# Key and value projections of a fused decoder layer in pairs of seven block products instead of eight, both values ahead of the second HGRN2 head

## The chip, the cores and the metric

One core of a Trainium2 chip runs the whole program in one launch. The metric is the time of that launch in microseconds (us). Times are medians of runs; a profiled execution is one run with the hardware profiler, and its trace gives start and length of every instruction. The engines are TensorE (PE, matrix products; PEld are its weight loads), VectorE (DVE), ScalarE (ACT), GpSimd (POOL) and SyncE (SP, which here issues nearly all transfers).

## The reference, cut to what matters

One layer of a hybrid decoder for 512 prompt tokens and 8 x 4 sample tokens (the sample tokens with caches of 2048 positions). All 544 tokens share the weights:

```
h = rmsnorm(x, norm_mix)
z = h @ w_in                                   # 1024 -> 3 * 512 + 4 * 512
aq, ak, av, hq, hf, hi, hg = split(z)
att = head_rmsnorm(dilated_attention(aq, ak, av))     # 8 heads of 64
o   = hgrn2_recurrence(silu(hq), 1 - f, hi, log f)    # 4 heads of 128
x = x + concat([att, head_rmsnorm(o) * silu(hg)]) @ w_out
x = x + cross_attention(rmsnorm(x), memory)
x = x + (silu(causal_conv3(u @ w_gate)) * (u @ w_up)) @ w_down    # u = rmsnorm(x), 2816 wide
return rmsnorm(x), new keys, new values, states
```

All is in float32. The change is in the products that make `ak` and `av`, two of the seven parts of `z`.

## The kernel before

Activations lie with features on the partitions and the 544 tokens along a row. A float32 product is made of three passes in a faster 32-bit format (`float32r`): every operand is split into a high part (ACT casts it) and a low part (DVE subtracts the high part from the original), and `passes` issues high x high, high x low and low x high, dropping low x low. For the norm's input these are `xs` (`xm0h`, `xm0l` to `xm7h`, `xm7l`, 128 features each, already times the gain `norm_mix`); the division by the norm's root, `r_mix`, is done when a result is evacuated, so projections can start before the norm is known.

A projection makes one tile of 128 output columns (two attention heads or one HGRN2 head): `proj_in` calls `dense`, which takes the next weight tile (`wr` raw, `wh` high, `wl` low, 1024 x 128 numbers as 8 blocks), and does the tokens in two halves, `CUTS`: 256 and 288 columns. Each half has a PSUM bank from `PD` (two banks), 8 x 3 matmuls and an evacuation on DVE by `proj_evac`. Behind each half `sides.pump()` lets one step of the side work be issued: the sample tokens' attention over the caches (`decode_attention`, whose tiles `st` come from memory through five buffers, with products `psd` for scores and `psdo` for values) and later the memory's input. Other small PSUM tiles come from `PX` (five banks). The softmax and value products of the prompt's attention (`prompt_attention`, tiles `psS`, `P`, `PT`, `psT`, `psO`) follow a value tile; `hgrn` follows the four projections of a head, with many small steps over levels of 1 to 64 tokens (`kq`, `hf`, `hG`, `psA`, `psB`, `psL`).

The order of the mixer is a tuple:

```
MIX_ORDER = (("h", 0), ("q", 0), ("q", 1), ("q", 2), ("q", 3), ("k", 0), ("k", 1), ("k", 2), ("k", 3), ("v", 0),
             ("h", 1), ("v", 1), ("h", 2), ("v", 2), ("h", 3), ("v", 3))
```

It is the order of writing alone. `tile_decoder_step` does not issue instructions: a recording layer, `Tape`, takes every instruction with an estimated length, groups them into steps, and `Tape.order` lays the steps out for each engine by a simulation with due times. The projections are the main line, in the order written (`tape.main()`); all else is put between them as it becomes ready and due, at most so far ahead as a gate on the main line allows. `tape.early(lead)` gives the steps within it an earlier due time. Because every instruction passes through one helper, nearly all rows of the profile have the line L723, and transfers L695; pieces of work are known by the names of their tiles. In the profile a tile's number is left out (`wl`, not `wl7`).

The feed-forward part, later, already does pairs of weight tiles with seven block products instead of eight (class `Pair`, banks `ps_a`, `ps_c`, `ps_d`, copies `kept`, sums `S1` to `S4` of weight blocks and `X`, `T`, `U`, `V` of token blocks). The mixer does not.

## Time and profile before

| | us |
|---|---|
| median of 3 runs | 821.66 (821.13 to 822.02) |
| the profiled execution | 821.08 |
| its span in the trace | 819.3 |
| PE busy | 808.6 |
| DVE busy | 594.8 |
| ACT busy | 421.3 |
| POOL busy | 152.9 |

The granted PE clock was 0.997 over the span. The span runs from the first to the last instruction; the execution's time is 1.8 us longer. Busy time counts overlapping instructions of one engine once. In the trace's rows the first number is the start in us from the span's beginning, the second the length; "[0.47 <-ACT keptu L723]" means that the engine was idle for 0.47 us ahead and that ACT's work on `keptu` ended this. The mixer's projections and side work fill the time from about 24 to 280 us, the feed-forward part that from about 442 us on.

### The profile page before, as it was taken

How to read it: one execution, taken by the hardware profiler on the slowest of the kernel's cores; microseconds unless marked ns; L12 is line 12 of the kernel's file. 1: busy time of each engine (PE TensorE's matmuls, PEld its weight loads, DVE VectorE, ACT ScalarE, POOL GpSimd, SP SyncE). 2: the span in 40 equal slices, each digit the busy share in tenths (PEclk: the TensorE clock that was granted, in tenths of full speed). 3: DMA queues.
4: the chain of work that ended last, by engine and by line, in shares of the span. 5: the costliest groups of instructions: out<-in, count | busy, mean ns of one | idle time of the engine just before them, and what ended most of it. 6: DMA issues, size and time to landing. Idle time of an engine off the chain costs nothing.

```text
span 819.3 us, 18836 instructions
## 1 busy us (share of the span) xinstructions
PE 808.6 (99%) x7545; PEld 761.3 (93%) x7545; DVE 594.8 (73%) x1252; ACT 421.3 (51%) x838; POOL 152.9 (19%) x246
## 2 busy tenths in 40 slices
PE   9999999999999999999999999999999999999996
PEld 9998988987998789999889999999999999999995
DVE  6785534965787996573589999876677767879983
ACT  7413533634636646353555565554455544666553
POOL 1130000110120310231133331121020212221023
PEclk9999999999999999999999999999999999999998
DMA  8657779696942544252733374556455645776603
GB/s 311 214 143 219 261 233 312 210 320 210 304 131 91 188 134 153 78 173 73 222 126 112 66 190 129 136 139 176 122 141 149 165 126 130 180 193 169 147 4 110
DMA packets 93639, 137.04 MB, mean 167 GB/s; under 512 B 6512, under 2 KB 60656, under 8 KB 93552
## 3 DMA queue, kind: packets, MB, share of 16 engines
q1 hardware_dynamic: 86496, 123.77, 47.5%
q0 software_dynamic: 6336, 11.54, 8.9%
q8 instruction: 59, 0.97, 0.5%
q10 hardware_dynamic: 720, 0.53, 0.2%
q14 instruction: 28, 0.23, 0.1%
HBM read 127.75 MB, written 8.07 MB: 166 GB/s over the span
## 4 chain that ended last, share of the span: by engine, by line
PE 95%; ACT 1%; DVE 1%; DMA 1%; SPq 0%; issue 0%; DVEq 0%
PE ps_d L723 9%; PE ps_au L723 7%; PE ps_ag L723 7%; PE ps_wo L723 6%; PE ps_cu L723 4%; PE ps_cg L723 3%; PE ps_k L723 3%; PE ps_q L723 3%; PE ps_hv L723 3%; PE ps_g L723 3%; PE ps_cq L723 3%; PE ps_v L723 3%; PE ps_dz L723 3%; PE ps_co L723 3%; PE ps_az L723 2%; PE ps_hq L723 2%
## 5 line engine op out<-in xcount | busy, mean ns | idle before, releaser
L723 ACT CAST wh<-wr 128x1024 fp32r<-128x1024 f32 (+1 forms) x68 | 59.4, 883 | 100.9 <-PE ps_q L723 15.4
L723 DVE TENSOR_TENSOR wl<-wr,wh 128x1024 fp32r<-128x1024 f32 (+1 forms) x68 | 71.6, 1062 | 8.3 <-ACT wh L723 7.7
L723 POOL TENSOR_TENSOR hG<-hG,hf 128x256 f32<-128x256 f32 (+1 forms) x28 | 24.4, 870 | 185.6 <-DVE hf L723 86.5
L723 POOL COPY last<-ug 128x2 f32<-128x2 f32 (+1 forms) x44 | 21.0, 500 | 128.0 <-DVE ug L723 107.3
L723 DVE TENSOR_TENSOR xr<-xr,ps_d 128x256 f32<-128x256 f32 (+1 forms) x48 | 20.9, 436 | 29.9 <-PE ps_d L723 29.8
L723 DVE SCALAR_TENSOR_TENSOR cv<-ug,vec,cv 128x560 f32<-128x560 f32 x44 | 35.1, 798 | 3.7 <-ACT cv L723 3.1
L723 ACT ACTIVATE cv<-cv 128x560 f32<-128x560 f32 x22 | 14.8, 673 | 17.8 <-DVE cv L723 17.7
L723 POOL TENSOR_TENSOR acc_cx<-acc_cx,sq_cx 128x256 f32<-128x256 f32 (+1 forms) x14 | 11.7, 837 | 58.5 <-ACT sq_cx L723 58.4
L723 ACT ACTIVATE P<-P,mx 128x128 f32<-128x128 f32 (+3 forms) x32 | 17.6, 553 | 9.1 <-DVE mx L723 8.9
L723 ACT ACTIVATE cv<-ug,vec 128x560 f32<-128x560 f32 x22 | 18.8, 857 | 4.2 <-DVE ug L723 3.2
L723 POOL COPY ug<-conv_state 128x16 f32<-128x16 f32 x22 | 17.3, 787 | 15.4 <-PE ps_au L723 9.1
L723 PE MATMUL ps_co<-coh,wh 128*128 128x256 f32 (+1 forms) x64 | 19.2, 300 | 0.1
L723 DVE TENSOR_TENSOR xr<-xr,ps_wo 128x256 f32<-128x256 f32 (+1 forms) x16 | 6.8, 436 | 16.3 <-PE ps_wo L723 16.3
L723 PE MATMUL ps_co<-col,wh 128*128 128x256 f32 (+1 forms) x64 | 18.4, 288 | 0.0
L695 POOL DMA_DIRECT2D S1u<-in_w_up x10 | 8.8, 877 | 51.7 <-DVE cv L723 26.2
L723 PE MATMUL ps_co<-coh,wl 128*128 128x256 f32 (+1 forms) x64 | 18.4, 288 | 0.0
L723 DVE TENSOR_TENSOR up<-ps_cu,keptu 128x272 f32<-128x272 f32 x20 | 8.7, 437 | 11.5 <-PE ps_cu L723 11.2
L723 PE MATMUL psd<-st,qbd_win 128*32 128x224 f32 x256 | 15.5, 358 | 0.0
L723 DVE CUSTOM_DVE_ANT_0 P<-psS,bias 128x128 f32<-128x128 f32 (+3 forms) x32 | 14.3, 485 | 1.2 <-PE psS L723 1.2
L723 POOL TENSOR_TENSOR acc_ux<-acc_ux,sq_ux 128x256 f32<-128x256 f32 (+1 forms) x13 | 11.3, 871 | 20.3 <-ACT sq_ux L723 20.1
L723 PE MATMUL psdo<-st,dpt 128*32 128x256 f32 x224 | 14.8, 385 | 0.0
L723 ACT ACT_TABLE_LOAD x11 | 14.1, 1283 | 1.4 <-PEq L2531 1.2
(2610 smaller groups left out, 3596.8 us busy)
## 6 DMA issues: line engine op xcount, KB each, us to landing
st<-in_kwT SPq DMA_DIRECT2D x32, 448.0 KB, 5.6
st<-in_vw SPq DMA_DIRECT2D x28, 512.0 KB, 6.5
wr<-in_w_in SPq DMA_DIRECT2D x25, 512.0 KB, 5.2
wd<-in_w_down SPq DMA_DIRECT2D x24, 256.0 KB, 3.2
wru<-in_w_up SPq DMA_DIRECT2D x10, 512.0 KB, 5.1
wrg<-in_w_gate SPq DMA_DIRECT2D x9, 512.0 KB, 4.9
st<-in_mkT SPq DMA_DIRECT2D x8, 512.0 KB, 5.2
wr<-in_w_out SPq DMA_DIRECT2D x8, 512.0 KB, 3.8
```

The costliest lines, as they stand in the source:

```text
L695: return tape.put(engine, lambda: call(*args, **kw), outs, ins, 0.1, 0.3, size)
L723: return tape.put(engine, lambda: call(*args, **kw), outs, ins, length, lag, size, port, codes, work, mode)
```

## The change

Two things. First, the mixer's order: keys 2 and 3 become one entry, values 0 and 1 become one, and both values stand ahead of the second HGRN2 head; value 1 stood behind that head.

Second, an entry with two tiles goes through `proj_pair`. With the two weight tiles as rows (A11 and A12: the two halves of the inner dimension of the first tile, A21 and A22: of the second) and the normed input as blocks (B11, B12: the first 512 features for tokens 0 to 271 and 272 to 543; B21, B22: the other 512 features), the 2 x 2 block product is made from seven products of 128 x 512 by 512 x 272, each 4 x 3 matmuls of 272 columns, in place of eight. The other operands are sums: S3 = A11 + A21, S1 = A21 + A22, S2 = S1 + A11 and S4 = S2 + A12 of weights, and X = B12 - B22, T = B11 - B12, U = X - B11 and V = B21 + U of tokens. Banks: a and c are the two `PD` banks, d comes from `PX`, and gets one marking matmul that opens its accumulation. ACT copies three partial results out of bank a while they are still to be added to (to d, to `z`, to `r`). `make_blocks` makes the token sums once, written after the first query tile with a lead of 30 us: ACT scales the eight input tiles by `norm_mix`, DVE makes 16 differences of 272 columns, ACT and DVE split them. `take_pair` makes the weight sums: four DVE adds of 512 columns, and five splits of 512, beside the first tile's split of 1024, as before.

The diff, cut to its core:

```diff
-MIX_ORDER = (("h", 0), ("q", 0), ("q", 1), ("q", 2), ("q", 3), ("k", 0), ("k", 1), ("k", 2), ("k", 3), ("v", 0),
-             ("h", 1), ("v", 1), ("h", 2), ("v", 2), ("h", 3), ("v", 3))
+MIX = (('h', 0), ('q', 0), ('q', 1), ('q', 2), ('q', 3), ('k', 0), ('k', 1), ('k', 2, 3), ('v', 0, 1), ('h', 1), ('h', 2), ('v', 2), ('h', 3), ('v', 3))
+PREPARE, LEAD_X = 2, 30.0
...
+        def take_pair(self, name):
+            top = self.take()
+            raw = self.raw[self.i - 1][0]
+            a11, a12 = raw[:, 0:4, :], raw[:, 4:8, :]
+            t = {n: A(f"{n}_{name}", [128, 4, 128]) for n in ("S3", "S1", "S2", "S4")}
+            self.load(self.i)
+            low = self.raw[self.i][0]
+            self.i += 1
+            a21, a22 = low[:, 0:4, :], low[:, 4:8, :]
+            sums = (("S3", a11, a21), ("S1", a21, a22), ("S2", t["S1"], a11), ("S4", t["S2"], a12))
+            found = {"A11": top[0:4], "A12": top[4:8]}
+            for n, a, b in sums:
+                nc.vector.tensor_tensor(t[n], a, b, op=ALU.add)
+            for n, src in (("S3", t["S3"]), ("S2", t["S2"]), ("S1", t["S1"]), ("S4", t["S4"]), ("A22", a22)):
+                hi, lo = (A(f"{n}{p}_{name}", [128, 4, 128], F32R) for p in "hl")
+                nc.scalar.copy(hi, src)
+                nc.vector.tensor_tensor(lo, src, hi.bitcast(F32), op=ALU.subtract)
+                found[n] = [(hi[:, k, :], lo[:, k, :]) for k in range(4)]
+            return found
...
+    mix_blocks = {}
+    def make_blocks():
+        for j, name in enumerate(("B11", "B21", "B12", "B22")):
+            c0 = HT * (j // 2)
+            mix_blocks[name] = [tuple(t[:, c0:c0 + HT] for t in xs[4 * (j % 2) + k]) for k in range(4)]
+        for k in range(KT):
+            nc.scalar.activation(xin[k][:, :N], xin[k][:, :N], AF.Copy, scale=V("norm_mix", k))
+        for kp in range(2):
+            made = {n: A(f"x{n}{kp}", [128, 2, HT]) for n in "XTUV"}
+            for i in range(2):
+                top, low = xin[2 * kp + i], xin[4 + 2 * kp + i]
+                b11, b12, b21, b22 = top[:, :HT], top[:, HT:N], low[:, :HT], low[:, HT:N]
+                x_, t_, u_, v_ = (made[n][:, i, :] for n in "XTUV")
+                for out, a, b, op in ((x_, b12, b22, ALU.subtract), (t_, b11, b12, ALU.subtract),
+                                      (u_, x_, b11, ALU.subtract), (v_, b21, u_, ALU.add)):
+                    nc.vector.tensor_tensor(out, a, b, op=op)
+            for n in "XUTV":
+                hi, lo = (A(f"x{n}{p}{kp}", [128, 2, HT], F32R) for p in "hl")
+                nc.scalar.copy(hi, made[n])
+                nc.vector.tensor_tensor(lo, made[n], hi.bitcast(F32), op=ALU.subtract)
+                mix_blocks.setdefault(n, []).extend((hi[:, i, :], lo[:, i, :]) for i in range(2))
+    def proj_pair(names):
+        name, outs = names[0], [A(n) for n in names]
+        w = ws.take_pair(name)
+        a, c, d, kept = PD(f"ps_a{name}"), PD(f"ps_c{name}"), PX(f"ps_d{name}"), A(f"kept{name}")
+        z, r = kept[:, :HT], kept[:, HT:N]
+        def product(ps, wn, xn, first, mark=None):
+            with tape.main():
+                if mark is not None:
+                    nc.tensor.matmul(mark[:, :HT], w[wn][0][0], mix_blocks[xn][0][0], start=True, stop=True)
+                for k in range(4):
+                    (hi, lo), (xh, xl) = w[wn][k], mix_blocks[xn][k]
+                    for i, (l, x_) in enumerate(((hi, xh), (hi, xl), (lo, xh))):
+                        nc.tensor.matmul(ps[:, :HT], l, x_, start=first and k == 0 and i == 0, stop=k == 3 and i == 2,
+                                         skip_group_check=True)
+            if wn not in ("S1", "S4", "A12"):
+                sides.pump()
+        def difference(c0, sub):
+            out = outs[1][:, c0:c0 + HT]
+            nc.vector.tensor_tensor(out, c[:, :HT], sub, op=ALU.subtract)
+            ROWS_ON(nc).tensor_tensor(out, out, r_mix[:, c0:c0 + HT], op=ALU.mult)
+        product(a, "A11", "B11", True, d)
+        nc.scalar.copy(d[:, :HT], a[:, :HT])
+        product(c, "S3", "X", True)
+        product(a, "S2", "U", False)
+        nc.scalar.copy(z, a[:, :HT])
+        product(d, "A12", "B21", False)
+        proj_evac(outs[0], None, d, 0, HT)
+        product(a, "S1", "T", False)
+        nc.scalar.copy(r, a[:, :HT])
+        difference(HT, r)
+        product(a, "S4", "B22", False)
+        proj_evac(outs[0], None, a, HT, HT)
+        product(c, "A22", "V", False)
+        difference(0, z)
+        return outs
...
+    def each(kind, at, scale=None):
+        names = [f"{kind}{p}" for p in at]
+        return proj_pair(names) if len(at) > 1 else [proj_in(names[0], scale)]
...
-    def project_k(p):
-        k = proj_in(f"k{p}")
-        kT.append(k)
-        leave(kT_out[128 * p:128 * p + 128, :], k[:, :N])
-        nc.gpsimd.tensor_copy(knew[:, p, :], k[:, SEQ:N])
-        knew_in.append(p)
-    def project_v(p):
-        v = proj_in(f"v{p}")
-        leave(vT_out[128 * p:128 * p + 128, :], v[:, :N])
-        prompt_attention(p, qT[p], kT[p], v)
-    def project_hgrn(h):
-        f, q, gt = first if h == 0 else [proj_in(f"h{n}{h}") for n in "fqg"]
-        hgrn(h, f, q, gt, proj_in(f"hv{h}"))
-    for what, i in MIX_ORDER:
-        if what == "h" and i == 3:
+    def project_k(*at):
+        for p, k in zip(at, each("k", at)):
+            kT.append(k)
+            leave(kT_out[128 * p:128 * p + 128, :], k[:, :N])
+            nc.gpsimd.tensor_copy(knew[:, p, :], k[:, SEQ:N])
+            knew_in.append(p)
+    def project_v(*at):
+        vs = each("v", at)
+        for p, v in zip(at, vs):
+            leave(vT_out[128 * p:128 * p + 128, :], v[:, :N])
+        for p, v in zip(at, vs):
+            prompt_attention(p, qT[p], kT[p], v)
...
+    for n, (what, *at) in enumerate(MIX):
+        if n == PREPARE:
+            with tape.early(LEAD_X):
+                make_blocks()
+        if what in "hH" and at[0] == 3:
             mem_side = sides.add(memory_in())
```

`project_q` and `project_hgrn` change in form only; their products and their order among the other entries stay, but for value 1's place.

How the instructions stand now. Counts of program instructions: PE 5575 before and 5553 after, DVE 1189 and 1237, ACT 778 and 808, POOL 249 and 248, SP 349 and 349. PE's order is the same up to the end of the third query tile.

PE, the key tiles, before: the end of key tile 2's first half and the start of its second (`xm7h` and `xm7l` are the eighth feature block, `wh7` and `wl7` key 2's weights).

```order
L723 MATMUL ps_k2_0_255<-xm7h_98,wh7_253 128x256
L723 MATMUL ps_k2_0_255<-xm7l_99,wh7_253 128x256
L723 MATMUL ps_k2_0_255<-xm7h_98,wl7_254 128x256
L723 MATMUL ps_k2_256_258<-xm0h_84,wh7_253 128x288
L723 MATMUL ps_k2_256_258<-xm0l_85,wh7_253 128x288
L723 MATMUL ps_k2_256_258<-xm0h_84,wl7_254 128x288
```

After: the end of the product S1·T and the start of S4·B22, both in the keys' bank a (`ps_ak2`).

```order
L729 MATMUL ps_ak2_295<-xTh1_234,S1h_k2_289 128x272
L729 MATMUL ps_ak2_295<-xTl1_235,S1h_k2_289 128x272
L729 MATMUL ps_ak2_295<-xTh1_234,S1l_k2_290 128x272
L729 MATMUL ps_ak2_295<-xm4h_92,S4h_k2_291 128x272
L729 MATMUL ps_ak2_295<-xm4l_93,S4h_k2_291 128x272
L729 MATMUL ps_ak2_295<-xm4h_92,S4l_k2_292 128x272
```

Halves of 256 and 288 columns in two banks have become products of 272 columns; between the last row of S1·T and the first of S4·B22 stands no other PE work, and ACT's copy of the first result lies between them by dependence.

DVE, the same place, before: key 1's evacuation, key 3's low part, and behind it the first softmax steps of the prompt's attention (`P`, `mx`), which go on past key 2's evacuation.

```order
L723 TENSOR_TENSOR k1_242<-ps_k1_0_246,r_mix_108 128x256
L723 TENSOR_TENSOR k1_242<-ps_k1_256_249,r_mix_108 128x288
L723 TENSOR_TENSOR wl8_265<-wr8_263,wh8_264 128x1024
L723 ISA P000_287,mx000_289<-psS000_285,bias00_282 128x128
L723 ISA mx000_289 128x1
```

After, around the evacuations of the key pair (`ps_dk2` and `ps_ck2` are its banks; `xT`, `xU`, `xV` token sums, `..l` low parts, `S1_v0` and its like weight sums of the value pair).

```order
L729 TENSOR_TENSOR xTl1_235<-xT1_227,xTh1_234 128x544
L729 TENSOR_TENSOR xV1_229<-x_6_82,xU1_228 128x272
L729 TENSOR_TENSOR xV1_229<-x_7_83,xU1_228 128x272
L729 TENSOR_TENSOR xVl0_225<-xV0_217,xVh0_224 128x544
L729 TENSOR_TENSOR wl9_311<-wr9_309,wh9_310 128x1024
L729 TENSOR_TENSOR xVl1_237<-xV1_229,xVh1_236 128x544
L729 TENSOR_TENSOR k2_275<-ps_dk2_297,r_mix_108 128x272
L729 TENSOR_TENSOR S3_v0_312<-wr9_309,wr10_316 128x512
L729 TENSOR_TENSOR S1_v0_313<-wr10_316 128x512
L729 TENSOR_TENSOR k3_276<-ps_ck2_296,keptk2_298 128x272
L729 TENSOR_TENSOR S2_v0_314<-S1_v0_313,wr9_309 128x512
```

The softmax steps have left this place; low parts and sums for the two pairs stand there, in front of the reads of the banks.

SP, the transfers around the key tiles' weights (`wr8` belongs to key 3, `wr9` and `wr10` to the next two tiles), before:

```order
L695 DMA wr8_263<-in_w_in 128x1024
L695 DMA st9_256<-in_kwT 128x4x224
L695 DMA wr9_272<-in_w_in 128x1024
L695 DMA out_ss_out<-hst00_186 128x4x128
L695 DMA st10_257<-in_kwT 128x4x224
L695 DMA out_ss_out<-hst01_187 128x4x128
L695 DMA out_st_out<-hS0_199 128x128
L695 DMA out_kT_out<-k0_231 128x544
L695 DMA st11_259<-in_kwT 128x4x224
L695 DMA st12_261<-in_kwT 128x4x224
L695 DMA bias00_282<-in_cst 128x512
```

After:

```order
L701 DMA st9_299<-in_kwT 128x4x224
L701 DMA st10_300<-in_kwT 128x4x224
L701 DMA wr8_284<-in_w_in 128x1024
L701 DMA out_ss_out<-hst00_186 128x4x128
L701 DMA out_ss_out<-hst01_187 128x4x128
L701 DMA out_st_out<-hS0_199 128x128
L701 DMA out_kT_out<-k0_255 128x544
L701 DMA st11_301<-in_kwT 128x4x224
L701 DMA st12_303<-in_kwT 128x4x224
L701 DMA wr9_309<-in_w_in 128x1024
L701 DMA wr10_316<-in_w_in 128x1024
```

The stream tiles `st9` and `st10` stand ahead of key 3's weights now, and the two weights of the value pair go one behind the other; the attention's bias tiles (`bias00`, `bias01`) go later.

More of the change, by code (lines that the diff above doesn't have):

```diff
@@ L41, with ROWS_ON @@
 LAST_PAIRS = 3
+def ROWS_ON(nc):
+    return nc.vector
 LEAD_T, LEAD_W = 20.0, 24.0
@@ L786, in tile_decoder_step @@
     specs = []
-    for what, i in MIX_ORDER:
-        if (what, i) == ("h", 0):
+    for what, *at in MIX:
+        if (what, at[0]) == ("h", 0):
             specs.append(w_in[20])
             continue
-        specs += [w_in[c + i] for c in {"q": (0,), "k": (4,), "v": (8,), "h": (16, 12, 24, 20)}[what]]
+        specs += [w_in[c + i] for i in at for c in {"q": (0,), "k": (4,), "v": (8,)}.get(what, (16, 12, 24, 20))]
     specs += [w_ck[i] for i in range(4)]
@@ L1588, in tile_decoder_step, with project_hgrn @@
     kT = []
-    def project_k(p):
-        k = proj_in(f"k{p}")
-        kT.append(k)
-        leave(kT_out[128 * p:128 * p + 128, :], k[:, :N])
-        nc.gpsimd.tensor_copy(knew[:, p, :], k[:, SEQ:N])
-        knew_in.append(p)
-    def project_v(p):
-        v = proj_in(f"v{p}")
-        leave(vT_out[128 * p:128 * p + 128, :], v[:, :N])
-        prompt_attention(p, qT[p], kT[p], v)
-    def project_hgrn(h):
-        f, q, gt = first if h == 0 else [proj_in(f"h{n}{h}") for n in "fqg"]
-        hgrn(h, f, q, gt, proj_in(f"hv{h}"))
-    for what, i in MIX_ORDER:
-        if what == "h" and i == 3:
+    def project_k(*at):
[10 more added lines that the diff above has]
+            prompt_attention(p, qT[p], kT[p], v)
+    def project_hgrn(what, h):
+        names = [f"h{n}{h}" for n in "fqg"] + [f"hv{h}"]
+        if h == 0:
+            f, q, gt, v = first + [proj_in(names[3])]
+        elif what == "H":
+            f, q, gt, v = proj_pair(names[:2]) + proj_pair(names[2:])
+        else:
+            f, q, gt, v = [proj_in(n) for n in names]
+        hgrn(h, f, q, gt, v)
+    for n, (what, *at) in enumerate(MIX):
[3 more added lines that the diff above has]
+        if what in "hH" and at[0] == 3:
             mem_side = sides.add(memory_in())
         if what == "q":
-            project_q(i)
-            if i == 3:
+            project_q(*at)
+            if 3 in at:
                 decode = sides.add(decode_attention())
         elif what == "k":
-            project_k(i)
+            project_k(*at)
         elif what == "v":
-            project_v(i)
+            project_v(*at)
         else:
-            project_hgrn(i)
+            project_hgrn(what, *at)
     sides.drain(mem_side)
```

## The prediction

> **What bounds the kernel now.** I read the page first (busy times, then the chain that ended last), then busy time in stretches around the changed place, then the list of waits, then single instructions.
>
> ```profile
> PE 808.6 (99%) x7545; PEld 761.3 (93%) x7545; DVE 594.8 (73%) x1252; ACT 421.3 (51%) x838; POOL 152.9 (19%) x246
> ...
> PE 95%; ACT 1%; DVE 1%; DMA 1%; SPq 0%; issue 0%; DVEq 0%
> ```
>
> PE works 808.6 of 819.3 us, and 95% of the chain that sets the end is PE. So time goes down only when PE's own list gets shorter, and up whenever another engine makes PE wait. The stretches show where that could be (from:to, length, then busy us of PE, weight loads, DVE, ACT and POOL, clock, DMA share, GB/s):
>
> ```profile
> 54.00:61.00 7.00, 7.00 (x68) 6.39 (x58) 6.84 (x15) 0.85 (x5) 2.15 (x4) 1.00 0.56 147
> ...
> 61.00:70.00 9.00, 8.98 (x95) 7.32 (x95) 6.25 (x18) 2.33 (x5) 1.34 (x2) 1.00 0.75 198
> 70.00:82.00 12.00, 12.00 (x124) 9.88 (x122) 4.95 (x9) 4.46 (x8) 0.21 (x1) 1.00 0.72 228
> 82.00:96.00 14.00, 14.00 (x140) 12.27 (x139) 8.24 (x34) 5.97 (x17) 0.42 (x2) 1.00 0.71 227
> ...
> 112.00:200.00 88.00, 88.00 (x1111) 73.30 (x1110) 50.25 (x137) 37.85 (x74) 7.38 (x10) 1.00 0.83 266
> 200.00:260.00 60.00, 60.00 (x733) 53.08 (x732) 45.19 (x118) 32.16 (x68) 7.67 (x10) 1.00 0.65 202
> 260.00:280.00 20.00, 19.30 (x172) 16.69 (x172) 18.75 (x57) 19.05 (x43) 2.15 (x2) 1.00 0.56 176
> 480.00:750.00 270.00, 269.93 (x2151) 269.71 (x2149) 210.09 (x379) 152.75 (x283) 52.63 (x110) 1.00 0.59 153
> ```
>
> The key tiles lie at 67 to 100 us. PE has no idle there, and DVE half of its time. The clock is full, so cycles are not at stake. Between 260 and 280 us DVE and ACT are nearly full, and PE loses 0.7 us, the only idle of these stretches to speak of. The feed-forward part (480 to 750) is PE and nothing else; whatever PE gains before it arrives at the end whole.
>
> **The products.** Four tiles (key 2 and 3, value 0 and 1) leave the plain form, in which each takes 24 matmuls of 256 columns and 24 of 288. Two pairs come, each of seven products of 12 matmuls of 272 columns, and one marking matmul. The feed-forward part has such products already, so both prices stand in the chain (start, us, what):
>
> ```profile
> 25.74 6.01 PE ps_hv L723 x48
> ...
> 92.62 1.78 PE psd L723 x48
> 94.40 6.22 PE ps_k L723 x48
> ...
> 511.91 1.51 PE ps_au L723 x12
> ```
>
> An undisturbed tile costs 6.01 us (6.22 behind a side trip, which I count below), a product 1.51. Removed: 4 x 6.01 = 24.04. Added: 14 x 1.51 = 21.14, and two marks of 1.51 / 12 = 0.13, together 21.40. PE's list shrinks by 2.64 us.
>
> **Fewer side trips.** Between the projections PE does attention and HGRN2 pieces in other array shapes. What a trip costs stands at its edges:
>
> ```profile
> 78.94 0.28 PE L723 MATMUL ps_k<-xm7l,wh 128*128 128x256 f32 x1
> 79.06 0.28 PE L723 MATMUL ps_k<-xm7h,wl 128*128 128x256 f32 x1
> 79.27 0.96 PE L723 MATMUL psd<-st,qbd_win 128*32 128x224 f32 x16
> ...
> 82.10 0.40 PE L723 MATMUL ps_k<-xm0h,wh 128*128 128x288 f32 x1
> 82.34 0.29 PE L723 MATMUL ps_k<-xm0l,wh 128*128 128x288 f32 x1
> ```
>
> Within the tile the next start comes after 0.12 us, into the trip after 0.21; back in a tile after 0.24, where 0.13 is the step. So a trip costs 0.2 us beside its own work, and 6.22 - 6.01 says the same. The order of the changed kernel merges trips: from the end of the third query tile to the output projection, projections and memory products stand in 34 unbroken runs where there were 40. Six fewer are worth 1.2 us; if two of them cost nothing, 0.8. I take 1.0.
>
> **A new wait between two products.** In a pair, S1·T and S4·B22 go into one bank: ACT must copy the first result out before the second is added. For the values, the order puts scores and decode work between the two. For the keys nothing stands there. The trace has one such place bare, at the end of the feed-forward part:
>
> ```profile
> 749.64 0.29 PE L723 MATMUL ps_au<-Th,S1u20l 128*128 128x272 f32 x1
> 750.41 0.39 PE L723 MATMUL ps_au<-B22h,S4u20h 128*128 128x272 f32 x1 [0.47 <-ACT keptu L723]
> 750.63 0.29 PE L723 MATMUL ps_au<-B22l,S4u20h 128*128 128x272 f32 x1
> ...
> 749.97 0.39 ACT L723 COPY keptu<-ps_au 128x272 f32<-128x272 f32 x1 [0.33 <-PE ps_au L723]
> ```
>
> The next start comes after 0.77 us instead of 0.12, and the one after it 0.09 late (0.22 for 0.13): 0.74 us. ACT was free there. Here its list grows by 10 casts of 512, 6 copies of 272, 8 scalings and 8 casts of 544, less two full casts. The nearest prices:
>
> ```profile
> 71.96 0.66 ACT L723 ACTIVATE hsq<-ho 128x544 f32<-128x544 f32 x1
> ...
> 74.39 1.04 ACT L723 CAST wh<-wr 128x1024 fp32r<-128x1024 f32 x1 [1.77 <-PE ps_k L723]
> ```
>
> That makes 26 steps of at most 0.66 and 6 of 0.39, less 2.08: under 17.5 us, spread over 40 to 110 us, where ACT idles for more than half of each stretch. So the wait stays near its bare size. Bounds: 0 (side work slips in) and 1.8 (a full cast of 1.04 stands ahead); taken 0.74.
>
> **DVE.** It gains the most: 16 block sums of 272 columns, 8 low parts of 544, 8 weight sums and 10 low parts of 512, 4 more evacuation steps of 272; it loses two low parts of 1024. Prices (the last two rows are groups: total, mean ns, then idle ahead):
>
> ```profile
> 59.09 0.42 DVE L723 TENSOR_TENSOR hf<-hf 128x256 f32<-128x256 f32 x1
> ...
> 59.62 0.72 DVE L723 TENSOR_TENSOR hq<-hq,hf 128x544 f32<-128x544 f32 x1
> 60.26 1.22 DVE L723 TENSOR_TENSOR wl<-wr,wh 128x1024 fp32r<-128x1024 f32 x1
> ...
> L723 DVE TENSOR_TENSOR S2u<-S1u,wru 128x512 f32<-128x512 f32 x10 | 6.8, 684 | 0.0
> ...
> L723 DVE TENSOR_TENSOR wl<-wr,wh 128x1024 fp32r<-128x1024 f32 x42 | 53.4, 1271 | 6.1 <-ACT wh L723 5.9
> ```
>
> Rows overlap by 0.08 us (0.72 long, but the next start after 0.64), so a step holds DVE for 0.36 (272, from the 256 row), 0.64, 0.60 or 1.14 us. Added: 16 x 0.36 + 8 x 0.64 + 18 x 0.60 + 4 x 0.36 - 2 x 1.14 = 20.8 us. Two block sums (0.72) fall into the full stretch 54 to 61, ahead of the first HGRN2 head; the rest goes to 61 to 100, where 35 - 6.25 - 4.95 - 8.24 = 15.6 us are free to 96. It fits because the value pair's 9 sums and low parts (5.4 us) come later, and value 0's softmax moves behind the key pair. Still, DVE runs without a pause through the key pair.
>
> Does PE feel it? The tight place is A22·V. It adds to the bank from which DVE must first have read S3·X, and that read stands behind key tile 1's last evacuation (0.4) and 20 more steps: six of 544 (3.84), nine of 272 (3.24), one of 1024 (1.14), two of 512 (1.2), a decode reduction (0.6, my estimate): 10.0, with the evacuation and the read itself 10.8 us. PE needs between the same ends the mark, six products, 28 decode matmuls (24 of them are the 1.78 above, so 2.1) and the wait of 0.74: 0.13 + 9.06 + 2.1 + 0.74 = 12.0. DVE is ahead by 1.2 us, if it gets to that evacuation in time. Up to there the 42 splits of the trace lost 5.9 us waiting for ACT, 0.14 each; 18 new ones could lose 2.5, which would leave PE waiting 1.3. The value pair has side work between its products and less to prepare; 0.9 more for it makes the upper bound 2.2. The lower is 0. PE's waits from 60 to 480 us, in the whole list, are these two:
>
> ```profile
> PE psT L723 <- ACT PT L723: 0.5, 1, 0.5
> PE ps_ck L723 <- DVE v L723: 0.2, 1, 0.2
> ```
>
> I take 0.5, nearer to the end that these rows show.
>
> The port between DVE and POOL could speak against the change:
>
> ```profile
> 39.21 0.97 POOL L723 TENSOR_TENSOR hG<-hG,hf 128x272 f32<-128x272 f32 x1
> ...
> 39.35 1.91 DVE L723 TENSOR_TENSOR wl<-wr,wh 128x1024 fp32r<-128x1024 f32 x1
> ```
>
> The same split that takes 1.22 elsewhere took 1.91 beside POOL's product. From 61 to 96 us POOL is busy for 1.34 + 0.21 + 0.42 = 2.0 us, so DVE could lose up to 2.0 us more there; less the lead of 1.2, PE could wait 0.8. I count nothing, because POOL's long steps (1.34) stand at 64 us, far ahead of the tight place. The Trainium skill, page "SBUF — State Buffer", section "Who interferes with whom", says that a DVE instruction with two SBUF inputs contends with a GpSimd instruction that reads SBUF, and that the second to issue waits it out; the 1.91 agrees. By that rule nearly every added sum and low part is exposed, and the sum below would be worse by those 0.8 us.
>
> **DMA and the queues.** 349 transfers before and after. On SP, two stream tiles now stand ahead of key tile 3's weights.
>
> ```profile
> wr<-in_w_in SPq DMA_DIRECT2D x25, 512.0 KB, 5.2
> ...
> 61.50 0.34 SPq L695 DMA_DIRECT2D wr<-in_w_in  x1
> ...
> 75.98 0.94 SPq L695 DMA_DIRECT2D st<-in_kwT  x2
> ```
>
> Those weights go out at 61.5 now. The two tiles need the decode rows at the head of HGRN2's memory part, near 62 us, so the weights leave by 64 and land by 69; the pair's second product wants its sums at 84. The next two stream tiles (76.0, then some 5 us) are wanted 28 decode rows deep, at 86, no earlier than they come. Decode then runs some 5 us ahead of now, against a DMA share of 0.71 to 0.83. Bounds 0 and 1; PE waits for no stream in the list above, so 0. POOL's copies of the new keys come at the pair's end, ahead of the decode rows that read them: 0. The 0.7 us idle at 260 to 280 may go, as value 1's softmax leaves that part; counted as 0.
>
> **Sum.** -2.64 - 1.0 + 0.74 + 0.5 = -2.4 us. The profiled execution took 821.08 us (span 819.3), so 818.7; the median of the runs is 821.66, 0.6 above it, and from there 819.3. I say 818.8.
>
> **Rivals.** (1) DVE binds both pairs: its wait at 2.2, the keys' bank wait at 1.8. -2.64 - 1.0 + 4.0 = +0.4: 821.4 from the profiled execution, 822.0 from the median. For it: DVE without pause for 25 us. Against: one wait on DVE, 0.2 us, in 420 us of trace. Chance 0.17. (2) The port: 0.8 us on top of my sum, 819.5 to 820.1, at the edge of no change; for it the 1.91, against it POOL's few steps. Chance 0.04. (3) Slower: with both values first, HGRN2 head 1's level products come five half tiles (15 us) later and run into head 2 and value 2, at 200 to 260 us, where DVE has 15 of 60 us free. If DVE fills there as at 260 to 280, PE loses 0.7 us per 20 us, 2.1 in all; one chain of level steps bare, ten of the 0.42 above, adds 4.2. It decides when PE loses over 4.0 us there (-2.4 + 4.0 = +1.6): 823 to 825. Against: value 1's attention leaves that part. Chance 0.10. (4) More than I count: the 0.7 idle goes, trips give 1.2, no DVE wait: 817.3 to 817.9, a better end of my own forecast.
>
> **Chances.** A measurement of this kernel tells about 0.2% (1.6 us) from no change, so faster needs under 820.0. The forecast with rival 4, 817.0 to 820.0, has 0.69. Rivals 1 and 2 make no change, 0.21 together. Slower: 0.10. The range, 816.9 to 821.7, reaches to rival 1 and leaves out the slower case and rival 1's upper end.
>
> **What would show it.** Right: PE busy about 3.5 us shorter; 14 products near 1.5 us each; one wait of the keys' a bank on ACT, near 0.5 in the list; 1 us or less of new PE idle between 61 and 120 us. Wrong: PE waits on DVE at the keys' c bank or on low parts of U, T or V; decode products that wait for streams; PE idle between 200 and 260 us.

## The result, and the profile after

| | before | after |
|---|---|---|
| median of the runs, us | 821.61 (821.13 to 822.02, 4 runs) | 816.70 (816.18 to 816.77, 4 runs) |
| the profiled execution, us | 821.08 | 816.77 |
| its span, us | 819.3 | 815.0 |

The ratio is 0.9939 with a 95% interval of 0.9922 to 0.9956: 4.9 us faster by the medians, 4.3 us by the spans. Forecast were 818.8 us and a range from 816.9. The direction was right, the gain 2 us larger than said, and the time 0.2 us below the range.

The page of the changed kernel, busy times and chain:

```profile
PE 804.8 (99%) x7523; PEld 759.2 (93%) x7523; DVE 613.4 (75%) x1296; ACT 434.8 (53%) x868; POOL 160.5 (20%) x246
...
PE 96%; DVE 1%; ACT 1%; DMA 1%; SPq 0%; issue 0%; DVEq 0%
```

PE is still everything. It is busy for 3.8 us less, DVE for 18.6 us more (20.8 were counted), ACT for 13.5 more. The stretches (PE, weight loads, DVE, ACT, POOL busy us, clock, DMA share, GB/s):

```profile
70.00:82.00 12.00, 12.00 (x102) 11.08 (x101) 12.00 (x23) 7.62 (x14) 4.21 (x1) 1.00 0.56 180
82.00:96.00 14.00, 13.53 (x145) 12.18 (x144) 13.60 (x28) 7.38 (x14) 1.25 (x2) 1.00 0.69 234
...
200.00:260.00 60.00, 60.00 (x743) 51.59 (x743) 49.10 (x135) 33.60 (x74) 8.12 (x10) 1.00 0.67 206
260.00:280.00 20.00, 20.00 (x218) 17.48 (x218) 16.89 (x40) 12.54 (x27) 3.40 (x3) 1.00 0.62 190
480.00:745.00 265.00, 265.00 (x2112) 264.94 (x2111) 203.85 (x368) 147.69 (x277) 52.37 (x108) 1.00 0.60 152
```

DVE has gone from 4.95 of 12 and 8.24 of 14 to 12.00 and 13.60: it works without pause through the key tiles, as forecast, and PE still loses only 0.47 us there. At 260 to 280 us the 0.7 us of PE idle are gone. The key pair in the chain, from its mark to its last product, and the only wait of PE between 26 and 318 us in the list:

```profile
82.24 0.12 PE ps_dk L729
82.37 1.52 PE ps_ak L729 x12
83.88 1.51 PE ps_ck L729 x12
...
92.31 0.40 ACT keptk L729
...
92.74 1.77 PE ps_ak L729 x12
94.52 1.51 PE ps_ck L729 x12
...
PE ps_ak L729 <- ACT keptk L729: 0.5, 1, 0.5
```

The products cost 1.51 us each. The bare place between S1·T and S4·B22, instruction by instruction:

```profile
91.98 0.29 PE L729 MATMUL ps_ak<-xTh,S1l_k 128*128 128x272 f32 x1
92.74 0.39 PE L729 MATMUL ps_ak<-xm4h,S4h_k 128*128 128x272 f32 x1 [0.47 <-ACT keptk L729]
92.97 0.29 PE L729 MATMUL ps_ak<-xm4l,S4h_k 128*128 128x272 f32 x1
```

The step is 0.76 us for 0.12 and the next 0.1 late: what was read from the feed-forward part before.

**Where the 4.33 us of the span are.** Both traces can be cut at the same two instructions: the first matmul of the first head's value (`ps_hv`) and the first of the output projection (`ps_wo`). Ahead of the first cut after is 0.21 us earlier, behind the second the two are alike (502.36 and 502.39 us). Between them it took 291.38 us before and 287.23 after: 4.15 us. The projections' products are 2.66 of it (192 matmuls less, 170 more; by the lengths in the chain, four tiles of 6.01 go, 14 products of 1.51 and two marks of 0.12 come), the idle at 260 to 280 us is 0.58, the bare wait gives 0.64 back. There remain 1.55 us. They are a remainder, which I put at the edges between pieces of PE work; the table of all laying-outs below tests this.

### The profile page after: what moved, and what is told of

Its sections match the earlier page's. It is cut to its first block, busy times and chain, and to the rows that moved or that the text cites. A ratio compares the mean times of both kernels' runs of the same rounds, so it can differ in the third digit from the quotient of the medians.

```text
span 815.0 us, 18856 instructions
## 1 busy us (share of the span) xinstructions
PE 804.8 (99%) x7523; PEld 759.2 (93%) x7523; DVE 613.4 (75%) x1296; ACT 434.8 (53%) x868; POOL 160.5 (20%) x246
## 4 chain that ended last, share of the span: by engine, by line
PE 96%; DVE 1%; ACT 1%; DMA 1%; SPq 0%; issue 0%; DVEq 0%
PE ps_d L729 9%; PE ps_au L729 7%; PE ps_ag L729 7%; PE ps_wo L729 6%; PE ps_cu L729 4%; PE ps_cg L729 3%; PE ps_q L729 3%; PE ps_hv L729 3%; PE ps_g L729 3%; PE ps_cq L729 3%; PE ps_dz L729 3%; PE ps_co L729 3%; PE ps_az L729 2%; PE ps_hg L729 2%; PE ps_hf L729 2%; PE ps_hq L729 2%
## 5 line engine op out<-in xcount | busy, mean ns | idle before, releaser
L729 ACT CAST wh<-wr 128x1024 fp32r<-128x1024 f32 (+1 forms) x66 | 57.0, 880 | 86.9 <-issue 14.9
L729 DVE TENSOR_TENSOR wl<-wr,wh 128x1024 fp32r<-128x1024 f32 (+1 forms) x66 | 69.1, 1061 | 12.4 <-ACT wh L729 11.7
L729 POOL COPY ug<-conv_state 128x16 f32<-128x16 f32 x22 | 19.1, 868 | 14.3 <-PE ps_au L729 5.8
L729 DVE TENSOR_TENSOR ug<-ps_cg,keptg 128x240 f32<-128x240 f32 (+2 forms) x27 | 8.5, 342 | 9.9 <-PE ps_cg L729 9.9
```

The source lines that it names most:

```text
L729: return tape.put(engine, lambda: call(*args, **kw), outs, ins, length, lag, size, port, codes, work, mode)
```

## The experiments

In each, "window" is the time between the two cuts, and "changes" counts, in the order in which the kernel is laid out, how often consecutive matmuls of this window differ in the array's rows or columns (in steps of 32, 64, 128) or in the number format.

**The new order alone**, and each pair alone, in the old order or the new.

```diff
-MIX = (..., ('k', 1), ('k', 2, 3), ('v', 0, 1), ('h', 1), ('h', 2), ('v', 2), ('h', 3), ('v', 3))
+MIX = (..., ('k', 1), ('k', 2), ('k', 3), ('v', 0), ('v', 1), ('h', 1), ...)   # order alone, PREPARE = -1
+MIX = (..., ('k', 1), ('k', 2, 3), ('v', 0), ('h', 1), ('v', 1), ('h', 2), ...)   # keys, old order
+MIX = (..., ('k', 1), ('k', 2), ('k', 3), ('v', 0, 1), ('h', 1), ...)   # values
+MIX = (..., ('k', 1), ('k', 2, 3), ('v', 0), ('v', 1), ('h', 1), ...)   # keys, new order
```

Expected of the order alone:

> The new order alone: both values ahead of the second HGRN2 head, all tiles in the plain form, no block sums. The products are those of before; the changes of array shape on PE from the first head's value to the output projection are 142 instead of 149, the unbroken projection runs 39 instead of 45. Theory A (each change of array shape costs about 0.14 us, and value 1's attention no longer fills DVE and ACT at 260 to 280 us, where 0.6 us of PE idle go): -7 x 0.14 - 0.6 = -1.6, so about 820.0 us. Theory B (the order is free, the whole gain belongs to the pairs): 821.6 us. Theory C (the later level products of head 1 collide): above 822 us, with PE idle between 200 and 260 us.

Measured: 820.38 us, ratio 0.9992 (0.9983 to 1.0001), window 290.94, PE idle in it 0.10. So the order gives 0.9 us by the medians (821.29 for the kernel before beside it) and 0.7 by the ratio, at most 1.4 by the interval. The interval just includes no gain, so theory B, a free order, is not excluded. Nothing collides at 200 to 260 us (theory C falls). The idle is gone as theory A had it, but the 1.0 us that theory A gave to fewer changes did not show.

Expected of the keys alone:

> Key tiles 2 and 3 as a pair, values plain, value 1 behind the second HGRN2 head as before; the token sums are made for this one pair. 142 changes of array shape instead of 149; scores stand between S1T and S4B22 here, so no bare wait. Theory A: -1.32 (one pair) - 7 x 0.14 = -2.3, 819.3 us, with the idle at 260 to 280 us still there. Theory D (a trip costs by unbroken projection run, 0.26 us each; 38 runs instead of 45): -1.32 - 1.8 = -3.1, 818.5 us.

Measured: 819.65 us, 0.9983 (0.9974 to 0.9992), window 289.75, no PE idle at all. Theory A's number is met within 0.4 us, D's missed by 1.2. But A's number is met by luck: it had the idle stay and the fewer changes give 1.0, and it is the idle that went, while the changes gave nothing (the table below has +0.4). The idle at 260 to 280 us went although value 1 stayed behind the head, so it was not value 1's attention, as I had thought. It comes with the laying-out: the kernel with the token sums alone, whose PE list is that of before, has it too.

Expected of the values alone:

> Value tiles 0 and 1 as a pair ahead of the second HGRN2 head, keys plain. 144 changes of array shape instead of 149, 39 runs instead of 45. Theory A: -1.32 - 5 x 0.14 - 0.6 (idle at 260 to 280 us gone) = -2.6, 819.0 us. Theory D: -1.32 - 6 x 0.26 - 0.6 = -3.5, 818.1 us. If the order cost something, above 819.5 us.

Measured: 819.16 us, 0.9975 (0.9966 to 0.9984), window 289.46. Theory A's 819.0 is met by number, D's 818.1 is not. Again the 0.7 us that A gave to fewer changes are not there: products and idle alone make 2.0 of the 1.9 us of window.

Expected of the keys in the new order:

> Key pair, both values plain but ahead of the second HGRN2 head: the changed kernel less the value pair, or the new order alone plus the key pair. Theory P (the pairs' products add up, 1.4 us each by the steps of the trace, and the rest is the place of the side work, which differs by up to 1 us from one laying-out to the next): 820.4 (order alone) - 1.4 = 819.0, give or take 1. Theory A (0.14 us per change of array shape, 148 here, 142 in the order alone): 819.0 + 0.8 = 819.8. Theory S (the two pairs need each other: 4.9 us together, 1.6 and 2.1 alone): near 820.

Measured: 818.96 us, 0.9973 (0.9964 to 0.9983), window 289.86. It is the 819.0 of theory P; theory A's 819.8 is missed by 0.8, and the pair's products need no partner.

**Other laying-outs of the same work.** The step of the decode attention, once in the kernel before and once in the changed one:

```diff
-TILES = (2, 2, 1)
+TILES = (3,)     # kernel before
+TILES = (2,)     # changed kernel
```

> The kernel before, but three stream tiles of the decode attention per step of side work instead of 2, 2, 1 in turn: the same instructions, put between the projections in another pattern. 159 changes of array shape instead of 149, 44 unbroken projection runs instead of 45. Theory A (0.14 us per change): +1.4, 823.0 us. Theory D (by projection run): -0.3, 821.3 us, no change.

Measured: 823.71 us, 1.0028 (1.0016 to 1.0039), window 294.90. Its list of PE's waits between the cuts begins with two that the kernel before has not, or has shorter:

```profile
PE ps_ck L723 <- DVE v L723: 1.0, 1, 1.0
PE psd L723 <- DMA st<-in_kwT: 0.5, 1, 0.5
```

Of the 3.5 us of window, 1.0 is new idle and 2.5 are left for the edges, with ten changes more and one projection run fewer. Theory D falls; theory A had 1.4 for the edges, 1.1 too little.

> The changed kernel with two stream tiles of the decode attention per step of side work each time instead of 2, 2, 1: the same instructions in another laying-out, 154 changes of array shape instead of 138, 43 unbroken projection runs instead of 39. Theory A (0.14 us per change): +2.2, 818.9 us. Theory P (the count says little; which piece stands at an edge and what it waits for does): within 1 us of 816.7, unless the list of waits names a wait.

Measured: 817.89 us, 0.9960 (0.9948 to 0.9973), window 288.71, no PE idle; the bare wait is filled here. With 16 changes more, the edges cost 2.1 us more than in the changed kernel (0.7 for -1.4 in the table below). That is theory A's 2.2 for them. Its time, 818.9, is still 1.0 too high, 0.6 of it the filled wait that it did not count; theory P's bound of 1 us is passed by 0.2.

**The token sums alone**, in the old order with plain tiles, made and used by nothing:

```diff
-MIX = (..., ('k', 1), ('k', 2, 3), ('v', 0, 1), ('h', 1), ('h', 2), ...)
+MIX = (..., ('k', 1), ('k', 2), ('k', 3), ('v', 0), ('h', 1), ('v', 1), ('h', 2), ...)
```

> The old order and plain tiles, but with the token sums made (and used by nothing): 16 sums of 272 and 8 low parts of 544 more on DVE (10.9 us), 8 scalings and 8 casts of 544 on ACT; PE's list is that of before, 149 changes of array shape. Theory F (all of it is covered): no change, 821.1 to 821.7. Theory L (it costs at the HGRN2 steps at 54 to 61 us or at the key tiles): over 822, with a wait of PE on DVE.

Measured: 820.60 us against 820.91 of the kernel before beside it, 1.0000 (0.9991 to 1.0008). The 10.9 us of DVE and some 10 of ACT are covered; the HGRN2 steps ahead of the key tiles don't feel them.

**How far DVE's cover reaches.** Low parts of token sums computed twice, for X and U or for all four:

```diff
                 nc.vector.tensor_tensor(lo, made[n], hi.bitcast(F32), op=ALU.subtract)
+                if n in "XU":                      # in the other run without this line
+                    nc.vector.tensor_tensor(lo, made[n], hi.bitcast(F32), op=ALU.subtract)
```

First the margin in the changed kernel, by DVE's rows: key 1's last evacuation, and the read of S3·X from the keys' c bank.

```profile
82.28 0.46 DVE L729 TENSOR_TENSOR k<-ps_k,r_mix 128x288 f32<-128x288 f32 x1
...
92.72 0.44 DVE L729 TENSOR_TENSOR k<-ps_ck,keptk 128x272 f32<-128x272 f32 x1
```

From the one's start to the other's end it is 10.88 us, for the 10.8 that the prediction counted; A22·V starts at 94.52, so DVE is ahead by 1.36.

> The changed kernel with only the four low parts of X and U computed twice: 4 more DVE steps of 0.64, 2.6 us, just ahead of and beside the key pair; PE's order there is unchanged, 139 changes of array shape instead of 138. Theory L (DVE is ahead by 1 to 1.4 us): key 1's last evacuation at about 82.9 still ahead of S3X (83.9), the low parts of U ready at 85.9 where PE wants them at 85.4, the keys' c bank read 0.5 to 1 us late: waits of PE on DVE of 0.5 to 1.2 us in all, 817.3 to 818.0, and no fall of the granted clock, since no wait is long. Theory F (wider cover): no wait, 816.7. Theory G (any wait of PE lets the clock fall as in the run with all eight doubled): over 819.

Measured: no wait of PE on DVE at the pair, which again takes 13.79 us from mark to end. The same two steps, and PE's first matmul of A22·V:

```profile
84.42 0.46 DVE L729 TENSOR_TENSOR k<-ps_k,r_mix 128x288 f32<-128x288 f32 x1
...
95.32 0.44 DVE L729 TENSOR_TENSOR k<-ps_ck,keptk 128x272 f32<-128x272 f32 x1
...
95.96 0.29 PE L729 MATMUL ps_ck<-xVh,A22h_k 128*128 128x272 f32 x1
```

The lead has shrunk from 1.36 to 0.20 us: 1.2 us for 2.6 us of steps. Theory L was right that DVE is pushed, but the wait of 0.5 to 1.2 us that it asked for did not come; that there is none is theory F's forecast, with 0.20 us to spare. The kernel as a whole is slower than the changed one, 819.62 us, 0.9984 (0.9975 to 0.9993), for reasons elsewhere. Its profiled execution, 821.70 us, is the slowest of its eleven, and there it reached the first cut 1.45 us later, its window is 1.42 us longer, of which 0.63 are a pause at 224 us, and its end is 2.07 us longer (504.46 us behind the second cut instead of 502.39). In the end part PE's order differs from the changed kernel's; it does so in this run and in the first run with the filled wait (below) alone, and these two alone have the longer end.

> The changed kernel with each of the eight low parts of the token sums computed twice: 8 more DVE steps of 0.64, 5.1 us, nearly all beside the key pair. Theory L (DVE is ahead of PE by only 1 to 1.4 us there): key 1's last evacuation starts near 86.0 instead of 82.3, and its bank is that of S3X, which started at 83.9: PE waits for DVE some 2.5 us at the keys' c bank; with 146 changes of shape instead of 138, 819 to 820.3. Theory F (DVE has room, the cover is wider than counted): no wait of PE on DVE in the list, 816.7 to 817.7.

Measured: 824.15 us, 1.0036 (1.0022 to 1.0050). The wait, the step that ends it, and three stretches around it:

```profile
PE ps_ck L729 <- DVE k L729: 3.9, 1, 3.9
...
88.50 0.45 DVE L729 TENSOR_TENSOR k<-ps_k,r_mix 128x288 f32<-128x288 f32 x1
...
83.00:85.00 2.00, 2.00 (x17) 1.84 (x15) 2.00 (x4) 0.12 (x1) 0.00 (x0) 1.00 0.58 227
...
89.00:92.00 3.00, 3.00 (x12) 2.76 (x12) 3.00 (x7) 1.21 (x2) 0.21 (x1) 0.50 0.24 93
92.00:95.00 3.00, 3.00 (x41) 1.69 (x44) 3.00 (x7) 1.87 (x3) 0.00 (x0) 0.50 0.24 45
```

Theory L's place is right (S3·X waits for key 1's bank), the wait is 1.4 us longer than said, and its time, 819 to 820.3, is passed by 3.9. What nobody had said is the last two rows: after 3.9 us without work PE's granted clock stood at 0.50 for 6 us, which by my estimate (half of the 6 us) makes some 3 us more. The cover is real and ends sharply.

**The bare wait filled.** A12·B21 of the key pair cut in two halves of 6 matmuls, the second between S1·T and S4·B22:

```diff
-        product(d, "A12", "B21", False)
-        proj_evac(outs[0], None, d, 0, HT)
+        product(d, "A12", "B21", False, ks=(0, 1))          # keys only
         product(a, "S1", "T", False)
         nc.scalar.copy(r, a[:, :HT])
+        product(d, "A12", "B21", False, ks=(2, 3))
+        proj_evac(outs[0], None, d, 0, HT)
```

> The changed kernel with the key pair's product A12B21 cut in two halves of 6 matmuls, one ahead of S1T and one between S1T and S4B22, so that ACT's copy lies beside PE work. Theory W (the bare wait costs 0.64 us of PE and nothing else): -0.64, no wait of PE on the keys' copy in the list; the laying-out has 142 changes of array shape instead of 138 and another place for the value pair's side work, worth at most 1 us either way: 816.1, between 815.1 and 817.1. Theory V (the wait moves: 6 matmuls are 0.76 us, about the length of the wait): two short waits in the list and 816.7.

Measured: 820.21 us, 0.9985 (0.9976 to 0.9994), 3.5 slower than the changed kernel. The pair itself went from 13.79 to 13.02 us, as theory W had it; its time, 817.1 at most, is missed by 3.1. The planner laid out other places anew: DVE makes all of the pair's weight sums ahead of key 0's evacuation, and the feed-forward part gets waits that the changed kernel has not. From the lists of waits:

```profile
PE ps_k L729 <- DVE k L729: 0.6, 1, 0.6
...
PE ps_du L729 <- ACT ps_du L729: 0.7, 1, 0.7
...
PE ps_az L729 <- DVE S4lz L729: 0.3, 1, 0.3
```

2.2 us are lost behind the second cut, 1.1 ahead of it. Two more laying-outs of the same cut, with the token sums due 45 and 60 us ahead (`LEAD_X` 45.0 and 60.0 for 30.0), keep the changed kernel's end:

> The same cut with the token sums due 45 us ahead; 139 changes of array shape, the end again that of the changed kernel, and key 1's last evacuation behind 2.4 us of other steps instead of 2.0. Theory W: 816.7 - 0.64 + 0.14 = 816.2, no wait on the keys' copy in the list, and the key pair from its mark to its last product some 0.7 us shorter than the 13.8 of the changed kernel. Theory V: 816.7 or more.

Measured: 816.05 us beside 820.91 of the kernel before, 0.9942 (0.9930 to 0.9955); span 814.0, window 286.61 instead of 287.23. PE's list of waits between the cuts is empty. The pair, mark to end, is 13.01 us:

```profile
81.89 0.12 PE ps_dk L729
...
89.65 1.50 PE ps_ak L729 x12
91.15 0.75 PE ps_dk L729 x6
91.91 1.50 PE ps_ak L729 x12
93.40 1.50 PE ps_ck L729 x12
```

> The cut of A12B21 again (the key pair's bare wait filled), with the token sums due 60 us ahead instead of 30, which gives a laying-out whose end is that of the changed kernel and not that of the first cut kernel; 137 changes of array shape. Two sums and a low part stand among the first HGRN2 head's level steps. Theory W (the wait is worth 0.64, and the first cut kernel lost 2.2 us at the program's end and 1.8 us ahead of the key tiles): 816.7 - 0.64 - 0.14 = 815.9, and after the output projection's start as long as the changed kernel (502.4). Theory V (filling the wait gains nothing here): 816.6 or more. If the head's level steps are late, PE waits on DVE between 45 and 62 us.

Measured: 816.00 us, 0.9936 (0.9923 to 0.9950), window 287.78. Here the wait is back, and longer, in spite of the half product:

```profile
PE ps_ak L729 <- ACT keptk L729: 0.8, 1, 0.8
...
92.33 0.62 ACT L729 CAST S3h_v<-S_v 128x512 fp32r<-128x512 f32 x1 [0.62 <-DVE S_v L729]
92.86 0.38 ACT L729 COPY keptk<-ps_ak 128x272 f32<-128x272 f32 x1
```

ACT's copy stands behind a cast for the value pair, whose weights landed late: the mechanism that the prediction named as this wait's upper bound. The casts' weights landed at 89.3 and 91.1 us; in the changed kernel they landed at 82.2 and 84.9. Theory W's 815.9 is met by luck here, for the wait that it had filled is there. So filling the wait is worth 0.6 to 0.8 us where it stands, which the profile shows and the times don't separate: the ratios of these two and of the changed kernel overlap.

**Due times.** The changed kernel with another lead:

```diff
-PREPARE, LEAD_X = 2, 30.0
+PREPARE, LEAD_X = 2, 10.0
```

> The changed kernel with the token sums due 10 us ahead instead of 30: the sums of X stand behind the first HGRN2 head's steps, at about 70 instead of 54 us; same PE order through the key pair; 135 changes of array shape instead of 138. Theory A: -3 x 0.14 = -0.4, 816.3 us, no new wait. Theory L: the 1.44 us of sums that now stand at 70 us and later push key 1's evacuation by at most 0.7 us, still ahead of S3X: no wait either; if there is one, DVE has less room than counted.

Measured: 816.22 us, 0.9935 (0.9923 to 0.9948), window 286.50, no new wait. As theory A had it; the gain over the changed kernel is within the interval.

**Two more pairs**, the second HGRN2 head's four projections:

```diff
-MIX = (..., ('v', 0, 1), ('h', 1), ('h', 2), ...)
+MIX = (..., ('v', 0, 1), ('H', 1), ('h', 2), ...)
```

> The changed kernel with the four projections of the second HGRN2 head as two more pairs (the token sums are there already): 2 x 1.33 us of products less; 148 changes of array shape instead of 138, +1.4; side work stands between S1T and S4B22 in both, so no new bare wait; DVE gets 18 more steps of 0.6. Theory A (products and changes of shape): -2.66 + 1.4 = -1.3, 815.4 us. Theory L2 (DVE late there, or the head's level steps too late): PE waits on DVE in the list between 110 and 290 us, 816.7 or more.

Measured: 822.71 us, 1.0012 (1.0003 to 1.0021). Theory A is missed by 7.3 us. Theory L2's sign came, a wait of PE on DVE at 120 us and a time over 816.7, but not its reason: DVE was not late with work. The softmax step for which PE waits had DVE standing idle for 4.1 us ahead of it, by the releaser that the profile names for a value tile's way out to memory; then the clock fell:

```profile
PE psS L729 <- DVE mx L729: 2.3, 1, 2.3
...
119.06 0.56 DVE L729 CUSTOM_DVE_ANT_0 P<-psS,bias 128x384 f32<-128x384 f32 x1 [4.11 <-DMA out_vT_out<-v]
...
119.70:122.00 2.30, 2.30 (x6) 0.68 (x10) 1.41 (x8) 2.25 (x10) 0.00 (x0) 0.50 1.06 401
122.00:125.00 3.00, 3.00 (x18) 2.41 (x11) 1.16 (x6) 1.94 (x6) 0.00 (x0) 0.50 0.82 239
```

The DMA share was above 1.0 there. That a buffer held by the transfer was waited for is likely and was not tried apart.

**The edges, over all laying-outs.** For each trace: the window, less the idle that the trace shows, plus 1.33 us for each pair, against the kernel before. The third column counts the changes of the array's rows or columns alone, without those of the number format. The two runs in whose window the granted clock fell to 0.50 (all low parts twice, and two more pairs) are left out.

| kernel | changes | of array shape | pairs | window | idle | rest against before |
|---|---|---|---|---|---|---|
| lead 10 | 135 | 97 | 2 | 286.50 | 0.48 | -2.0 |
| cut, lead 60 | 137 | 98 | 2 | 287.78 | 1.16 | -1.4 |
| the changed kernel | 138 | 99 | 2 | 287.23 | 0.59 | -1.4 |
| cut, lead 45 | 139 | 104 | 2 | 286.61 | 0.11 | -1.5 |
| X, U twice | 139 | 106 | 2 | 288.65 | 1.10 | -0.5 |
| cut | 142 | 110 | 2 | 288.37 | 0.62 | -0.3 |
| order alone | 142 | 112 | 0 | 290.94 | 0.10 | +0.2 |
| keys, old order | 142 | 112 | 1 | 289.75 | 0.00 | +0.4 |
| values | 144 | 113 | 1 | 289.46 | 0.00 | +0.1 |
| keys, new order | 148 | 116 | 1 | 289.86 | 0.10 | +0.4 |
| before | 149 | 110 | 0 | 291.38 | 0.70 | 0.0 |
| token sums alone | 149 | 110 | 0 | 291.70 | 0.90 | +0.1 |
| TILES (2,) | 154 | 119 | 2 | 288.71 | 0.00 | +0.7 |
| before, TILES (3,) | 159 | 124 | 0 | 294.90 | 1.67 | +2.6 |

A line through the 14 points rises by 0.15 us for each change (standard error 0.02), with 0.5 us of scatter; the order alone stands 0.7 us above it, the keys in the old order 0.9. Changes of array shape alone fit better: 0.14 us for each (standard error 0.01), 0.4 us of scatter, and those two lie within 0.2 us of the line.

The traces show the same step by step. Where the array shape changes, the next matmul starts 0.14 to 0.15 us later than by the mean step of the shape and format that it follows, in each of the 16 traces; where only the number format changes, it starts no later. Before, 110 changes of shape add 15.8 us in this way, after, 99 add 14.6. So 1.2 of the 1.55 us are seen at these places; the other 0.35 are not.

The single parts have 112, 112 and 113 changes of shape and the kernel before 110, where the whole has 99: this is why the single parts gained 0.9, 1.6 and 2.1 us and the whole 4.9. (The keys in the new order have 116, and gained 2.2.) Why the planner comes to fewer changes only with both pairs is not shown.

## Why the prediction was right and wrong

The mechanism held. PE's list got shorter, and the signs that were named for it came: PE is busy for 3.8 us less (3.5 were said), the products take 1.51 us, the one new wait is 0.47 us in the list, and PE has no other new idle. What failed is the size of three terms of the sum, each by about 0.5 us and all in the same direction: fewer side trips (-1.0 said, -1.55 in the account), DVE (+0.5 said, 0 measured) and the idle at 260 to 280 us (put at 0, -0.58 measured). Rival 4 had allowed for the last two. Fewer side trips is the one that goes past its own bounds, 0.8 to 1.2, and with it the time past the range: at 1.2 the time would be some 817.05.

- **The products.** Said -2.64, measured -2.66. The row of the feed-forward part (1.51) held in the mixer.
- **Fewer side trips.** Said -1.0, bounds 0.8 and 1.2; measured -1.55 (-1.4 in the table, which leaves the part of the bare wait that is no visible idle, 0.17 us, among the edges). This is the term that was sized wrongly. I counted the unbroken runs of projections (six fewer) and priced a run's two edges at 0.2 us. Edges between two pieces of side work cost as well, and the layout has 11 changes of array shape fewer in all; at 0.15 each that is 1.65. The steps at these changes show 1.2 of it; the rest of the 1.55 is not placed. A price by runs (theory D) failed in three of three experiments.
- **The new wait.** Said 0.74; measured 0.64 on the step itself and 0.1 on the next, so 0.74 by the reading that was used there, in the place and on the copy that were named. (The account above has 0.64; with 0.74 its remainder is 1.65.)
- **DVE.** Said +0.5, measured 0. The count of the list was good to 0.1 us, and the lead of 1.2 us was 1.36. What I added for splits that wait for ACT (up to 2.5 us) did not come: from 61 to 96 us no split of DVE waits for ACT in the changed kernel's list of waits, since DVE had a backlog. The doubled low parts showed the edge: with 2.6 us more the lead at A22·V is 0.2, with 5.1 us more PE waits 3.9, at S3·X.
- **The idle at 260 to 280 us.** Said 0, measured -0.58. I had named the cause that might remove it, value 1's attention, and it was the wrong one: the key pair in the old order loses the idle too.
- **The port.** The collision came, but on the other side than in rival 2 (the first row is the kernel before):

```profile
75.12 0.21 POOL L723 COPY knew<-k 128x32 f32<-128x32 f32 x1 [9.15 <-DVE k L723]
...
75.69 4.21 POOL L729 COPY knew<-k 128x32 f32<-128x32 f32 x1 [9.34 <-DVE k L729]
...
82.80 0.64 POOL L729 COPY knew<-k 128x32 f32<-128x32 f32 x1 [2.90 <-DVE k L729]
...
79.11 0.72 DVE L729 TENSOR_TENSOR om0l<-ho,om0h 128x544 fp32r<-128x544 f32 x1
79.75 0.42 DVE L729 TENSOR_TENSOR k<-ps_k,r_mix 128x256 f32<-128x256 f32 x1
...
82.66 1.36 DVE L729 TENSOR_TENSOR xUl<-xU,xUh 128x544 fp32r<-128x544 f32 x2
```

POOL's copy of a new key took 0.21 us before and 4.21 now, beside DVE's unbroken row of six steps with two SBUF inputs, which kept their length. It ended at 79.90, right behind the start of a DVE step that takes one input from PSUM. In nine of the traces with pairs, this one among them, the copy took 4.2 to 5.6 us. The next copy got through sooner: 0.64 us, ending 0.15 us behind the start of the second of two such steps. PE has no wait on these copies. The Trainium skill's "SBUF — State Buffer", section "Who interferes with whom", has it that issue order decides who waits. This trace agrees that the copy, which came second, waits; that it goes on waiting through six steps is more than that.
- **The slower rival** (level steps of head 1 colliding at 200 to 260 us) did not come: PE is busy for 60.00 of 60.00 us there in the changed kernel, though DVE is busier (49.10 for 45.19).
- **The range.** How its low end came to 816.9 is not said in the prediction. The better bounds of its own terms with the idle gone, -2.64 - 1.2 + 0 + 0 - 0.7 = -4.5, give 816.5 from the profiled execution, so the range was narrower than the sum allowed. The sum of what was right (-2.66 + 0.64) and what was left at 0 or short (-0.58 and -1.55, and 0.21 at the start, which no part of the change touches) is -4.36 for the 4.33 of the spans. The planner's freedom, 0.4 to 0.5 us of scatter in this window alone, was in no term; the 0.2 us by which the time lies below the range is less than that.

## What to carry to other kernels

Where a planner lays out an instruction list, price a change by the whole list: count the changes of array shape over all of PE's work, not only at the pieces that are edited, and allow for half a microsecond of luck and for an end that is laid out anew. Full cover can be read from the trace before: add up the steps of the covering engine between two bank reads; here this sum was good to 0.1 us, and the lead that it left to 0.2. The waits forecast for a longer list were 0.5 us too many in one run and 1.4 too few in the other. When a local gain is confirmed in the trace but the time is worse, compare the two traces cut at the same instructions; the loss may be 500 us away.

## What the runs showed of the hardware

One pause of PE of 3.9 us, and one of 2.3 us, were each followed by 6 to 7 us at a granted clock of 0.50, so that by my estimate (half of that time) each cost some 3 us beside its own length; a pause of 0.98 us (before, with `TILES` (3,), at 274.8 us) left it at 1.00 in the stretch behind it:

```profile
275.50:278.00 2.50, 2.25 (x19) 2.29 (x20) 1.92 (x6) 2.50 (x9) 0.00 (x0) 1.00 0.94 367
```

The Trainium skill, "TensorE: Matmul & The Clock Gate", section "Part 1: The HAM clock gate (the "warmup" mystery)", gives the half rate after an idle window of about 3.4 us; here 2.3 us were enough.
